# Merge statistics in one group of products, and residual gate rows computed beside the first projections

## The chip, the cores and the metric

The kernel runs on one core of a Trainium2 chip. The core has TensorE (PE) for matrix products, VectorE (DVE), ScalarE (ACT) and GpSimd (POOL) for the rest, SyncE (SP), which issues the kernel's transfers here, and 16 DMA engines that carry them. Each of these works through its own instructions in order and waits on semaphores for the others. The metric is the device time of one execution in microseconds (us), as the median of the runs; the profile and its trace come from one execution more.

## The reference

One step of a one-layer decoder with two parallel branches, width 1024, for 512 prompt rows and 8 x 4 sample rows:

```python
shift, scale, gate = split(silu(c) @ w_cond + b_cond)
h = x * (1 + scale) + shift
qa, ka, va, za, qkv_b, zb, a_b, b_b, g_a, g_b = split(h @ w_in)
yA = combine_groups(dilated softmax attention, 3 head groups) * silu(za)
yB = rmsnorm(gated delta rule over 8 heads of 128) * silu(zb)
merged = sigmoid(g_a) * (yA @ w_branch_a) + sigmoid(g_b) * (yB @ w_branch_b)
x = layernorm(ALPHA * x + gate * (merged @ w_out))
```

`gate` is the residual gate: one row of 1024 values for the prompt and one for each of the 8 sample sequences (`c_prompt` and `c_sample` have nine rows together). `combine_groups` weighs the three groups' attention outputs by their shares of the softmax denominator; for that the kernel needs each query's maximum and sum of every group: the merge statistics. All is in float32.

## The kernel before, in words

The kernel doesn't issue its instructions in the order in which the Python text names them. Calls on the engine objects are recorded (class `Recorder`, L244); generator threads record their part piece by piece, taking turns by rank and due time (class `Threads`, L680: among the parts that are due, the one with the smaller rank goes first, and a `yield 4.0` asks to come back 4 us later by the planner's own count). Then `schedule` (L425) puts every engine's instructions in one fixed order with a cost model, and `emit` writes them; so every instruction of the trace shows line 670, and work is told apart by the names of its tiles. Operations recorded within `rec.together()` (L331) stay contiguous on their engine; others may have instructions of other threads put between them.

The main thread is `stream` (L905, rank 9): the input projections, then the branch products. A job is 48 matmuls, 8 blocks of the contraction times three passes of high and low parts (`hhi`, `hlo` by `hi`, `lo`) for each of two halves of 272 columns, into two PSUM banks `pp` in turn. The weights come as `wt` (512 KB) into three buffers; ACT makes `hi` and DVE `lo` from them. A bank comes free when its half is evacuated, for the gate jobs `za` and `zb` by a tanh on ACT and `zt<-zt,pp` on DVE. Beside the stream run the attention (`prompt_attention`, L1405), the delta rule of eight heads (tiles `kq`, `KQ`, `NTs`, `QKd`, `S`, `rc`, results `dO`), the sample rows, and copies of the caches (`out_kv_s`).

After the attention pairs j = 1 and j = 3, `prompt_attention` merges the groups (L1504 to L1540). It turns the statistics `st` into rows with 40 small products, each two records in the trace, into one bank `pt` (a `pg` bank): four kinds `kd` of statistics, in four strips of PE columns at 0, 32, 64 and 96 (`tile_position`). For each kind and each strip r, the even kinds have four products and the odd ones a single one. On DVE and ACT follows a chain over `R` and `Z` that ends in the weights `R`; these go to DRAM (`dw<-R`, L1527, four transfers) and come back broadcast over 64 partitions each (`wv<-dw`, L1534, eight transfers); `ya` and `NB` are multiplied by them and added (L1537 to L1539). The event `merged[j]` is set then, and the job `za` for j (L1867) starts on it.

The residual gate rows come from `gate_rows` (L1956), a thread of rank 1 that is added for the last phase (L2112), beside the branch products. It loads the bias rows into `gp` (128 equal rows for the prompt) and `gs` (64 rows for the samples), and for each half of 512 columns loads the gate's part of `w_cond` in four transfers of 512 KB (`wc`, from a pool of its own), multiplies it with the conditioning (`cs`) in two groups of 4 products, into a `pd` bank of 32 rows, copies it to `Y`, and spreads the rows with two selector products: `selc` for `gp`, `selg` for `gs`, with an addition on DVE after each. `gp` and `gs` are read in the layer's last stage (from L2153 on), which multiplies the output products with them.

The tiles named `o` (pool `op`, nine buffers of 128 x 544) hold, later on, the gate jobs' `zt`, `ybh` and the low parts `yal`.

Of the kernel before, what the change touches and what calls it, by code (L numbers as in the profile page):

```python
# [11 lines left out]
F32 = mybir.dt.float32  # L12
# [7 lines left out]
D = 1024  # L20
KT = 8
# [4 lines left out]
NT = SEQ + NS  # L26
# [48 lines left out]
def shape_constants():  # L75

    p = np.arange(128)
    b4, i4, h8 = p // 32, p // 8 % 4, p % 8
    blk = {}
    blk["ident"] = np.eye(128)  # L80
    blk["selc"] = (p[:, None] % 32 == np.arange(9)[None, :])
    tok = np.arange(2 * NS)
    blk["selg"] = (p[:, None] % 32 == 1 + tok[None, :] % NS // 4)
    blk["triu"] = (p[:, None] <= p[None, :])
    same = p[:, None] // 4 == p[None, :] // 4
    blk["btri"] = same & (p[:, None] <= p[None, :])
    blk["bones"] = same
    blk["low16"] = np.where(p[:, None] % 32 >= 16, -1.0, 0.0)
    blk["strict4"] = same & (p[:, None] < p[None, :])
    blk["dmask"] = np.where(p[:, None] <= p[None, :], 0.0, -BIG)  # L90
    blk["dmask_s"] = np.where(same & (p[:, None] <= p[None, :]), 0.0, -BIG)
    blk["bmask"] = (p[:, None] % 32 // 4 == np.arange(8)[None, :])
    blk["hmask"] = (p[:, None] % 4 == np.arange(4)[None, :])
    sab = np.zeros((128, 4, 4))
    for h4 in range(4):
        for g in range(2):
            sab[4 * g + h4::16, h4, g] = 1.0
            sab[8 + 4 * g + h4::16, h4, 2 + g] = 1.0
    blk["selab"] = sab.reshape(128, 16)
    blk["sel16"] = p[:, None] % 16 == np.arange(16)[None, :]  # L100
    cols, blobs = {}, []
    for names in (("ident", "selc", "selg", "low16", "dmask"), ("selab", "sel16", "triu", "btri", "bones"),
                  ("strict4", "dmask_s", "bmask"), ("hmask",)):
        at = 0
        for name in names:
            cols[name] = (at, blk[name].shape[1])
            at += blk[name].shape[1]
        blobs.append(np.ascontiguousarray(np.concatenate([blk[n] for n in names], axis=1), dtype=np.float32))
    return cols, blobs


CCOLS, CONST = shape_constants()
# [131 lines left out]
class Recorder:  # L244
# [20 lines left out]
    def pool(self, make, name, bufs, side):  # L265
        return Pool(self, make, name, bufs, side)
# [456 lines left out]
def body(ctx, tc, io):  # L723
    rec = Recorder()
    pe, ve, se, ge, sp = rec.engines()
    mv = sp
    threads = Threads(rec)

    pool = lambda stack, name, bufs, side="left": stack.enter_context(rec.pool(
        lambda: tc.tile_pool(name=name, bufs=bufs, side=side, reuse_waits="tile"), name, bufs, side))  # L730
# [12 lines left out]
    dram = ctx.enter_context(rec.pool(lambda: tc.tile_pool(name="dram", bufs=1, space=DRAM), "dram", 1, "dram"))  # L743

    def pg():
        return psg.tile([128, 512], F32, name="pg", tag="g")

    def pd():
        return psd.tile([128, 512], F32, name="pd", tag="d")
# [4 lines left out]
    def pp():  # L754
        return psp.tile([128, 512], F32, name="pp", tag="pp")


    cst = consts.tile([128, CONST[0].shape[1]], F32, name="cst")
    tables = {"early": cst}

    def take(gen, n):
        for _ in range(n):
            if next(gen, "end") == "end":
                return

    def C(name, where="early"):
        a, n = CCOLS[name]
        return tables[where][:, a:a + n]

    ident = C("ident")  # L770
# [11 lines left out]
    op = pool(octx, "opool", 9, "right")  # L782
# [12 lines left out]
    def cond_product(part, load, ps):  # L795


        for k, n, wc in load(part):
            q = (k + 2 * n) % 4
            pe.matmul(ps[n][32 * q:32 * q + 32, :], cs[:, k, :], wc, start=(k < 4), stop=(k >= 4),  # L800
                      tile_position=(0, 32 * q))
            yield

    def cond_rows(part, k0, nk):
        return io["w_cond"][k0 * 128:(k0 + nk) * 128, part * D:(part + 1) * D].rearrange("(k p) c -> p k c", p=128)

    def to_features(pv, k, rows):

        for i in range(4):
            pe.matmul(pv[:, k + i, 0:9], rows[:, 128 * i:128 * i + 128], C("selc"), start=True, stop=True)  # L810
# [16 lines left out]
    with ExitStack() as fctx:  # L827
# [36 lines left out]
        for part, t in ((1, sc), (0, sh)):  # L864
            ps = [pp(), pp()]
# [3 lines left out]
            for n in range(2):  # L869
                Y = fr.tile([128, 512], F32, name="Y", bufs=2)  # L870
                if n:
                    se.activation(Y, ps[n], AF.Copy)
                else:
                    ve.tensor_copy(Y, ps[n])
                to_features(pv, 4 * n, Y)
            if part:
# [94 lines left out]
    tail = d0.tile([128, 34], F32, name="tail")  # L971
    etot = d0.tile([128, 34], F32, name="etot")
    dO = dram.tile([8, 128, 512], F32, name="dO")
    qd = dram.tile([2, 2, NS, 256], F32, name="qd")
    us = d0.tile([128, 3, 8, NS], F32, name="us")
    oS = keep.tile([128, 8, NS], F32, name="oS")
# [428 lines left out]
    def prompt_attention():  # L1405

        for j in range(4):
            qt, kt, vrow = {}, {}, {}
            for g in range(3):
# [3 lines left out]
                pt = pg()  # L1413
# [4 lines left out]
                pt = pg()  # L1418
# [5 lines left out]
                for u, t in enumerate((krow, vrow[g])):  # L1424
                    if g == 0:
                        sp.dma_start(io["kv0_p"][:, u, cs_], t[:, 3])
                    else:
                        o = io[f"kv{g}_p"].rearrange("(n a r) u c -> a n r u c", a=4, r=4)
# [4 lines left out]
            if j % 2 == 0:  # L1433
                NB = ap.tile([128, 2, 512], F32, name="NB")
                st = ap.tile([128, 4, 4, 4], F32, name="st")
# [29 lines left out]
            for i in range(4):  # L1465
# [5 lines left out]
                for hh in range(2):  # L1471
                    pt = pg()
# [30 lines left out]

            pt = pg()  # L1504
            ve.memset(pt, 1.0)
            for kd in range(4):
                for r in range(4):
                    o = pt[32 * r:32 * r + 4, 128 * kd:128 * kd + 128]
                    if kd % 2:
                        pe.matmul(o, st[:, kd, r, :], ident, start=True, stop=True, tile_position=(0, 32 * r))  # L1510
                        continue
                    for i in range(4):
                        pe.matmul(o.rearrange("p (a n) -> p n a", a=4)[:, 8 * i:8 * i + 8, :], st[:, kd, i, :],
                                  ident[:, r:128:4], start=True, stop=True, tile_position=(0, 32 * r))
            R = ap.tile([128, 4, 128], F32, name="R", tag="P", bufs=2)
            Z = ap.tile([128, 4, 128], F32, name="Z", tag="P", bufs=2)
            two = lambda t: t[:, None, :].to_broadcast([128, 2, 128])
# [10 lines left out]
            for j2 in (j - 1, j):  # L1528
                wv = []
                for u in range(2):  # L1530
                    w = ap.tile([128, 512], F32, name="wv", tag="PT" if j2 < j else "P", bufs=2)
# [423 lines left out]

    def gate_rows():  # L1956

        b = io["b_cond"][:, 2 * D:]
        sp.dma_start(gp, b.to_broadcast([128, D]))
        sp.dma_start(gs, b.to_broadcast([64, D]))  # L1960
        ps = [pd(), pd()]
        yield 4.0
        for n in range(2):
            w = slice(512 * n, 512 * n + 512)

            for k0 in range(0, KT, 4):
                wc = []
                for k in (k0, k0 + 2):
                    wc.append(wcp.tile([128, 2, 512], F32, name="wc"))
                    sp.dma_start(wc[-1], cond_rows(2, k, 2)[:, :, w])  # L1970
                with rec.together():
                    take(cond_product(2, lambda part: ((k0 + k, n, wc[k // 2][:, k % 2]) for k in range(4)), ps), 99)
                yield 2.0
            Y = zp.tile([128, 512], F32, name="Y", tag="rbo")
            se.activation(Y, ps[n], AF.Copy)
            yield 1.8
            for t, r, sel in ((gp, 128, C("selc")[:, 0:1].to_broadcast([128, 128])), (gs, 64, C("selg"))):
                p = pg()
                pe.matmul(p[0:r], sel, Y, start=True, stop=True)
                ve.tensor_add(t[:, w], t[:, w], p[0:r])  # L1980


    for s in (1, 0, 2):
# [33 lines left out]
    def early():  # L2017
        yield freed[1], merged[1]
        t, slabs = early_tiles()
        sample_queries(0, slabs()[0:64, 0:256], t["qr"])  # L2020
        yield from sample_attention(0, t, slabs, 512, 6.0, (ve,), early_over)
        yield tuple(ready[3, g] for g in range(3))
        sample_queries(1, slabs()[0:64, 0:256], qr1)

    threads.add(early(), 4)

    def prep():
# [15 lines left out]
    zp = pool(zctx, "zp", 2, "right")  # L2043
# [32 lines left out]
    gp = al.tile([128, D], F32, name="gp")  # L2076
    gs = al.tile([64, D], F32, name="gs")
# [12 lines left out]
            se.activation(wo[n][0][:, k:k + 2], raw, AF.Copy)  # L2090
            ve.tensor_sub(wo[n][1][:, k:k + 2], raw, wo[n][0][:, k:k + 2].bitcast(F32))

    wctx = ExitStack()
    wcp = pool(wctx, "wcp", 3, "right")

    def merge_after(m):
        def after():
            t = gate_tile["ga", m]
# [10 lines left out]

    for m in range(8):  # L2110
        jobs += [gate_job("ga", m)] * (m >= EARLY_A) + [branch_job("ga", m, 4, of_a, after=merge_after(m))]
    threads.add(gate_rows(), 1)  # L2112
    threads.add(stream(len(jobs)), 9)
    threads.run(lambda: not threads.parts)
    wctx.close()
    zctx.close()
    gates_ctx.close()
    octx.close()
# [15 lines left out]
    r = [o1.tile([128, D], F32, name=f"r{tt}") for tt in range(5)]  # L2134
# [18 lines left out]
    for n in range(2):  # L2153
        for tt in (4, 0, 1, 2, 3):
# [8 lines left out]
            for c in range(512 * n, 512 * n + 512, step):  # L2163
                po = product_out(tt, c, c + step)
                w = slice(c, c + step)
# [15 lines left out]
            w, w2 = slice(0, m), slice(m, 1024)  # L2181
# [118 lines left out]
```

## Time and profile before

| what | value |
|---|---|
| runs | 942.03, 938.55, 942.79 us; median 942.03 |
| profiled execution | 939.77 us, its span 938.0 us |
| mean granted PE clock | 0.984 |
| moved by DMA | 237.76 MB, mean 253 GB/s |

How to read the rows of the trace: in the rows of the order of time stand the start in us from the span's start, the time of the row, engine, line, operation, what it writes and reads, its shape, how many instructions the row holds, and in brackets how long the engine had been idle and who released it. "SPq" rows are the issue of a transfer, not the transfer. Rows of waits have: who waited, for whom, us in all, times, the longest. A matmul's own time overlaps with that of the next, so that its cost is read from the distance of starts.

### The profile page before, as it was taken

To read this page: it belongs to the slowest core of one execution; us is meant where nothing else is said; L and a number is where in the kernel's file an instruction comes from. 1 tells how busy PE (TensorE), PEld (TensorE's weight loads), DVE (VectorE), ACT (ScalarE), POOL (GpSimd) and SP (SyncE) were. 2 spreads that over 40 slices of the span, in tenths; PEclk is the share of its full clock that TensorE was granted. 3 is DMA by queue.
4 is the path that set the end of the run, shared out by engine and by line. 5 is a ranking of instruction groups with operands and counts; after the bars stand their busy time and mean duration, and the time that the engine had idled before them with its cause. 6 is when DMAs were issued, how large, how long until landed. Compare 5 with 4: busy or idle time off the path is not lost.

```text
span 938.0 us, 20669 instructions
## 1 busy us (share of the span) xinstructions
PE 892.0 (95%) x8070; PEld 825.8 (88%) x8070; DVE 736.8 (79%) x1620; ACT 417.0 (44%) x975; POOL 64.0 (7%) x176
## 2 busy tenths in 40 slices
PE   4799999999999999999999998988999999999995
PEld 1599999999989999979999997877999999998784
DVE  1575556876799999889989997556899789957768
ACT  0365347753557443576725753441532222234411
POOL 0120000200011110010100200001020000000000
PEclk9799999999999999999999999998999999999998
DMA  9677773658878778786787868459689899988613
GB/s 357 226 220 238 221 246 136 224 182 251 272 249 273 229 250 287 236 292 219 241 301 242 277 206 298 140 172 365 219 267 360 340 418 377 361 284 306 205 43 112
DMA packets 106341, 237.76 MB, mean 253 GB/s; under 512 B 30898, under 2 KB 62140, under 8 KB 103556
## 3 DMA queue, kind: packets, MB, share of 16 engines
q1 hardware_dynamic: 106244, 236.45, 73.8%
q8 instruction: 63, 1.03, 0.4%
q14 instruction: 34, 0.28, 0.1%
HBM read 220.40 MB, written 103.70 MB: 346 GB/s over the span
## 4 chain that ended last, share of the span: by engine, by line
PE 72%; DVE 11%; DMA 4%; ACT 3%; issue 2%; SPq 0%; POOL 0%; DVEq 0%; POOLq 0%; ACTq 0%
PE pp L670 55%; PE pg L670 7%; PE pd L670 6%; PE pb L670 3%; DVE slab L670 2%; DMA dO<-orow 1%; DMA wv<-dw 1%; DMA slab<-in_vs 1%; DVE lo L670 1%; ACT L670 1%; DVE XF L670 1%; DVE r L670 1%; ACT hi L670 1%; DVE ya L670 1%; DVE acc L670 0%
## 5 line engine op out<-in xcount | busy, mean ns | idle before, releaser
L670 PE MATMUL pp<-hhi,hi 128*128 128x272 f32 x1408 | 415.6, 295 | 11.3 <-DVE zt L670 8.7
L670 PE MATMUL pp<-hhi,lo 128*128 128x272 f32 x1408 | 415.3, 295 | 0.0
L670 PE MATMUL pp<-hlo,hi 128*128 128x272 f32 x1408 | 414.1, 294 | 0.2 <-DVE small L670 0.2
L670 PEld LDWEIGHTS pp<-hhi,hi 128*128 128x128 f32 x1408 | 267.2, 190 | 13.7 <-DVE zt L670 9.1
L670 PEld LDWEIGHTS pp<-hlo,hi 128*128 128x128 f32 x1408 | 267.2, 190 | 2.7 <-issue 0.9
L670 PEld LDWEIGHTS pp<-hhi,lo 128*128 128x128 f32 x1408 | 266.5, 189 | 3.3 <-issue 1.8
L670 ACT ACTIVATE hi<-wt 128x1024 fp32r<-128x1024 f32 (+1 forms) x104 | 106.8, 1027 | 167.7 <-PE pp L670 144.8
L670 DVE TENSOR_TENSOR lo<-wt,hi 128x1024 fp32r<-128x1024 f32 (+1 forms) x104 | 122.5, 1178 | 54.8 <-ACT hi L670 54.0
L670 DVE SCALAR_TENSOR_TENSOR acc<-ext,cw,acc 128x568 f32<-128x568 f32 x72 | 57.5, 799 | 0.7
L670 ACT ACT_TABLE_LOAD x38 | 48.8, 1283 | 9.3 <-DMA cT<-in_cT 8.0
L670 DVE TENSOR_TENSOR slab<-slab 128x512 f32<-128x512 f32 (+1 forms) x66 | 42.4, 663 | 3.7 <-DMA slab<-in_vs 3.1
L670 DVE TENSOR_REDUCE slab<-slab 128x8 f32<-128x512 f32 (+2 forms) x66 | 42.4, 655 | 0.3
L670 ACT ACTIVATE P<-P,st 128x256 f32<-128x256 f32 (+1 forms) x64 | 31.3, 491 | 19.7 <-DVE st L670 19.5
L670 PE MATMUL pp<-ybl,hi 128*128 128x272 f32 x128 | 37.0, 289 | 0.0
L670 PE MATMUL pp<-ybh,lo 128*128 128x272 f32 x128 | 37.0, 289 | 0.0
L670 PE MATMUL pp<-ybh,hi 128*128 128x272 f32 x128 | 36.8, 288 | 0.0
L670 ACT ACTIVATE zt<-pp 128x272 f32<-128x272 f32 x48 | 18.4, 389 | 34.7 <-PE pp L670 31.7
L670 POOL COPY cx<-ext 128x3 f32<-128x3 f32 (+1 forms) x48 | 23.3, 515 | 94.0 <-ACT ext L670 93.9
L670 ACT ACTIVATE vn<-pd,beta 128x128 f32<-128x128 f32 x32 | 11.7, 366 | 34.4 <-PE pd L670 34.3
L670 DVE TENSOR_TENSOR Tb<-Tb,tmp 32x15 f32<-32x15 f32 (+7 forms) x120 | 23.4, 195 | 4.1
L670 PE MATMUL pp<-wc,cs 128*32 128x512 f32 x64 | 13.1, 916 | 14.3 <-DMA wc<-in_w_cond 14.3
L670 ACT ACTIVATE ext<-pp 128x272 f32<-128x272 f32 (+2 forms) x72 | 20.0, 314 | 14.9 <-PE pp L670 13.9
(395 smaller groups left out, 1574.3 us busy)
## 6 DMA issues: line engine op xcount, KB each, us to landing
out_kv_s<-in_cache SPq DMA_DIRECT2D x144, 512.0 KB
wt<-in_w_in SPq DMA_DIRECT2D x88, 512.0 KB
out_kv_s<-in_cache SPq DMA_DIRECT2D x24, 496.0 KB
wc<-in_w_cond SPq DMA_DIRECT2D x8, 1024.0 KB
slab<-in_ks SPq DMA_DIRECT2D x32, 256.0 KB
slab<-in_vs SPq DMA_DIRECT2D x32, 256.0 KB
kv<-in_ks SPq DMA_DIRECT2D x16, 512.0 KB
kv<-in_vs SPq DMA_DIRECT2D x16, 512.0 KB
```

The lines of the kernel that those rows point to most:

```text
L670: getattr(real[x.engine], x.name)(*map(arg, x.args), **{k: arg(v) for k, v in x.kw.items()})
```

## The change

The merge's 40 products are recorded within `rec.together()`, and the loops stand in another order: kind, product, strip, so that four successive products go to the four column strips in turn. The products themselves are the same.

`gate_rows` is added beside `early()`, before the first projections, as a thread of rank 5. For each half of the columns it loads the weights in eight transfers of 256 KB (`wg`) into `o` tiles that nothing else uses at that time, does the eight products in one group, and copies the result to `Y`. A single selector product of 73 columns (9 of `selc`, 64 of `selg`, which are neighbours in the constants) makes the rows of both kinds at once. The bias comes as a transfer that broadcasts one row of 512 values over 73 partitions (`grow`), DVE adds the product to it, and a transfer stores the 73 rows in a DRAM tile `dg`. At the place where the thread was added before, `gp` is loaded from `dg`'s first row, broadcast, and `gs` from its rows 9 to 72. The pool `wc` of the late weights is gone. From the removed lines on, line numbers are up to four smaller than before.

```diff
+    dg = dram.tile([73, D], F32, name="dg")
...
             pt = pg()
             ve.memset(pt, 1.0)
-            for kd in range(4):
-                for r in range(4):
-                    o = pt[32 * r:32 * r + 4, 128 * kd:128 * kd + 128]
-                    if kd % 2:
-                        pe.matmul(o, st[:, kd, r, :], ident, start=True, stop=True, tile_position=(0, 32 * r))
-                        continue
-                    for i in range(4):
-                        pe.matmul(o.rearrange("p (a n) -> p n a", a=4)[:, 8 * i:8 * i + 8, :], st[:, kd, i, :],
-                                  ident[:, r:128:4], start=True, stop=True, tile_position=(0, 32 * r))
+            with rec.together():
+                for kd, i in ((kd, i) for kd in range(4) for i in range(1 if kd % 2 else 4)):
+                    for r in range(4):
+                        o = pt[32 * r:32 * r + 4, 128 * kd:128 * kd + 128]
+                        if kd % 2:
+                            pe.matmul(o, st[:, kd, r, :], ident, start=True, stop=True, tile_position=(0, 32 * r))
+                        else:
+                            pe.matmul(o.rearrange("p (a n) -> p n a", a=4)[:, 8 * i:8 * i + 8, :], st[:, kd, i, :],
+                                      ident[:, r:128:4], start=True, stop=True, tile_position=(0, 32 * r))
...
     def gate_rows():
 
-        b = io["b_cond"][:, 2 * D:]
-        sp.dma_start(gp, b.to_broadcast([128, D]))
-        sp.dma_start(gs, b.to_broadcast([64, D]))
-        ps = [pd(), pd()]
-        yield 4.0
+        sel = cst[:, CCOLS["selc"][0]:CCOLS["selc"][0] + 73]
         for n in range(2):
             w = slice(512 * n, 512 * n + 512)
-
-            for k0 in range(0, KT, 4):
-                wc = []
-                for k in (k0, k0 + 2):
-                    wc.append(wcp.tile([128, 2, 512], F32, name="wc"))
-                    sp.dma_start(wc[-1], cond_rows(2, k, 2)[:, :, w])
-                with rec.together():
-                    take(cond_product(2, lambda part: ((k0 + k, n, wc[k // 2][:, k % 2]) for k in range(4)), ps), 99)
-                yield 2.0
-            Y = zp.tile([128, 512], F32, name="Y", tag="rbo")
+            wc = [op.tile([128, NT], F32, name="wg", tag="o")[:, 0:512] for _ in range(KT)]
+            for k in range(KT):
+                sp.dma_start(wc[k], io["w_cond"][128 * k:128 * k + 128, 2 * D + 512 * n:2 * D + 512 * n + 512])
+            ps = {n: pd()}
+            yield 6.0
+            with rec.together():
+                take(cond_product(2, lambda part: ((k, n, wc[k]) for k in range(KT)), ps), 99)
+            Y = op.tile([128, NT], F32, name="Y", tag="o")[:, 0:512]
             se.activation(Y, ps[n], AF.Copy)
-            yield 1.8
-            for t, r, sel in ((gp, 128, C("selc")[:, 0:1].to_broadcast([128, 128])), (gs, 64, C("selg"))):
-                p = pg()
-                pe.matmul(p[0:r], sel, Y, start=True, stop=True)
-                ve.tensor_add(t[:, w], t[:, w], p[0:r])
+            rows = op.tile([128, NT], F32, name="grow", tag="o")[0:73, 0:512]
+            sp.dma_start(rows, io["b_cond"][:, 2 * D + 512 * n:2 * D + 512 * n + 512].to_broadcast([73, 512]))
+            yield 3.0
+            p = pd()
+            pe.matmul(p[0:73], sel, Y, start=True, stop=True)
+            ve.tensor_add(rows, rows, p[0:73])
+            sp.dma_start(dg[:, w], rows)
+            yield 1.0
...
+    threads.add(gate_rows(), 5)
     threads.add(early(), 4)
...
-    threads.add(gate_rows(), 1)
+    sp.dma_start(gp, dg[0:1].to_broadcast([128, D]))
+    sp.dma_start(gs, dg[9:73])
     threads.add(stream(len(jobs)), 9)
     threads.run(lambda: not threads.parts)
-    wctx.close()
```

More of the change, by code (lines that the diff above doesn't have):

```diff
@@ L2091, in load_out @@
             ve.tensor_sub(wo[n][1][:, k:k + 2], raw, wo[n][0][:, k:k + 2].bitcast(F32))
-    wctx = ExitStack()
-    wcp = pool(wctx, "wcp", 3, "right")
     def merge_after(m):
```

## The prediction

> **What bounds the kernel now.** I read the page first, then PE's waits, the stretches around the longest one, and last the order of work on DVE and SP there.
>
> ```profile
> span 938.0 us, 20669 instructions
> PE 892.0 (95%) x8070; PEld 825.8 (88%) x8070; DVE 736.8 (79%) x1620; ACT 417.0 (44%) x975; POOL 64.0 (7%) x176
> ...
> PE pp L670 <- DMA wc<-in_w_cond: 14.3, 6, 10.6
> PE pp L670 <- DVE zt L670: 9.2, 2, 8.7
> ```
>
> PE is busy for 95% of the span. So whatever takes PE time away in a full stretch is a gain at its whole length, and whatever makes PE wait in one is a loss at its whole length. The first wait, 14.3 us, is the conditioning at the start, which the change doesn't touch. The second is one stall of 8.7 us:
>
> ```profile
> 627.67 1.02 PE L670 MATMUL pb<-kq 128*128 128x256 f32 x4
> 637.44 0.59 PE L670 MATMUL pp<-hhi,hi 128*128 128x272 f32 x1 [8.75 <-DVE zt L670]
> ...
> 637.40:641.00 3.60, 3.56 (x16) 3.56 (x17) 2.14 (x7) 0.00 (x0) 2.03 (x5) 0.50 1.14 348
> ...
> 81.00:96.00 15.00, 15.00 (x120) 14.88 (x119) 8.14 (x17) 4.77 (x9) 0.00 (x0) 1.00 0.65 208
> ```
>
> After it the granted clock is 0.50 for 3.6 us: 16 matmuls take 3.6 us, 0.225 each, where a full stretch at clock 1.00 has 120 in 15 us, 0.125 each: another 1.6 us. (The columns of such rows: the stretch and its length, busy time and count of PE, PEld, DVE, ACT and POOL, the granted clock, the DMA share, GB/s.) The stall with its tail costs 10.4 us. What DVE and SP did before it:
>
> ```profile
> 612.18 1.31 PE L670 MATMUL pg<-cst,st 128*4 128x32 f32 x32
> ...
> 619.81 0.43 DVE L670 TENSOR_TENSOR R<-R,Z 128x256 f32<-128x256 f32 x1
> 620.26 2.81 SPq L670 DMA_DIRECT2D dw<-R  x4
> 625.03 4.97 SPq L670 DMA_DIRECT2D wv<-dw  x8
> 630.54 1.02 DVE L670 TENSOR_TENSOR ya<-ya,wv 128x512 f32<-128x512 f32 x1 [0.48 <-DMA wv<-dw]
> 636.96 0.78 DVE L670 SCALAR_TENSOR_TENSOR zt<-zt,pp 128x272 f32<-128x272 f32 x2
> ```
>
> This is the second merge of the attention branch. The statistics products end at 613.49, DVE works out R until 620.24, R goes to DRAM and comes back broadcast, and the ya operations run from 630.54. The evacuation `zt<-zt,pp`, which frees PE's bank, stands behind them in DVE's order.
>
> **The change part by part. (1) Statistics products together.** Today the planner cuts the second merge's products into pieces over 9.2 us, with projections and delta-rule products between; the first merge's stay whole:
>
> ```profile
> 604.29 1.08 PE L670 MATMUL pg<-cst,st 128*4 128x32 f32 x28
> ...
> 608.96 0.28 PE L670 MATMUL pp<-hhi,lo 128*128 128x272 f32 x1
> 609.17 0.38 PE L670 MATMUL pg<-cst,st 128*4 128x128 f32 x2
> 609.48 0.49 PE L670 MATMUL pd<-S,KQ 128*128 128x128 f32 x2
> ...
> 306.38 2.65 PE L670 MATMUL pg<-cst,st 128*4 128x32 f32 x80
> ```
>
> From 608.96 to 609.48 are 0.52 us, of which the projection needs 0.125: a piece of two records costs 0.39. Whole, 80 records take 2.65 us, 0.07 for two. Four such pieces (I leave the longer ones' edges out) save 4 x 0.32 = 1.3 us.
>
> The larger part: begun at 604.29, the whole group ends at 606.94 and not at 613.49. R's chain, which hangs on it, moves 6.5 us ahead; the projections that stood between come behind it. PE's work up to the blocked matmul shrinks by the 1.3 us alone, so it blocks at about 628.7 - 1.3 = 627.4 and is freed at 637.44 - 6.5 = 630.9: 3.5 us instead of 8.75. A wait of that size stands earlier in the trace:
>
> ```profile
> PE pg L670 <- DVE st L670: 3.1, 1, 3.1
> ...
> 578.70:582.10 3.40, 3.30 (x30) 2.27 (x31) 2.87 (x11) 2.32 (x9) 0.00 (x0) 0.63 0.98 347
> ```
>
> It too has a tail: 3.4 us at 0.63, 1.3 us lost; I take 1.4. Gain 10.4 - 4.9 = 5.5. Bounds: R's way through DRAM took 10.3 us here, 620.24 to 630.54, but 14.4 in the first merge, where the reciprocal's product ended at 328.78 and `ya<-ya,wv` began at 343.17:
>
> ```profile
> 328.38 0.40 DVE L670 TENSOR_TENSOR R<-R,Z 128x256 f32<-128x256 f32 x1
> 343.17 1.07 DVE L670 TENSOR_TENSOR ya<-ya,wv 128x512 f32<-128x512 f32 x1 [0.54 <-DMA wv<-dw]
> ```
>
> With 4.1 us more the gain is 1.4; at most it is 10.4, the stall gone. The order of the products, with the four column strips in turn, leaves their number and sizes; the trace has no such order. If a group took half or twice its 2.65 us, the two merges would gain 2.7 or lose 5.3; I take nothing, since the pieces of today change strips too.
>
> **(2) Gate rows leave the late stage.** There PE is full, so its products count whole:
>
> ```profile
> 839.26 0.29 PE L670 MATMUL pp<-yah,hi 128*128 128x272 f32 x1
> 839.48 1.06 PE L670 MATMUL pd<-wc,cs 128*32 128x512 f32 x8
> 840.70 0.29 PE L670 MATMUL pp<-yah,lo 128*128 128x272 f32 x1
> ...
> 852.56 1.02 PE L670 MATMUL pg<-Y,cst 128*128 128x512 f32 x2
> ...
> 855.00:872.00 17.00, 17.00 (x123) 13.53 (x122) 12.39 (x22) 9.36 (x16) 0.00 (x0) 1.00 0.83 297
> ```
>
> A group of 8 records costs 840.70 - 839.26 - 0.25 = 1.19 us, four of them 4.8; the two records of a selector product take 1.02, four products 4.1. Removed: 8.9. The new place, beside the first projections, is as full (below), so there the products count whole too: two groups of 16 records, 2.2 each (two of 1.19 less one pair of edges), and two selector products with 73 columns, 1.02 each: 6.4, or up to 8.9 if each group is cut in two. Gain 2.5, at the least nothing. The `Y` copies on ACT, the additions on DVE and the late loads lay beside that full PE: nothing; at the new place the same holds for ACT (4.77 us busy of the 15 after 81.00), not for DVE's additions (3). `gp` and `gs` are read back from `dg` where PE is full, and are read only in the layer's last stage; without that cover 0.75 MB would show with about 2 us at the 407 GB/s below.
>
> **(3) The new transfers.** The eight loads of 512 KB late give way to sixteen of 256 KB early. The first eight fall where DMA has nothing to do, the next into a loaded stretch:
>
> ```profile
> 28.00:30.00 2.00, 1.02 (x8) 0.16 (x8) 0.29 (x1) 0.31 (x1) 0.72 (x4) 1.00 1.05 407
> ...
> 36.00:38.00 2.00, 1.87 (x8) 1.87 (x9) 2.00 (x7) 0.18 (x1) 0.07 (x1) 0.50 0.56 143
> 38.00:44.00 6.00, 6.00 (x42) 5.87 (x41) 5.09 (x10) 3.10 (x6) 1.10 (x3) 0.81 0.00 0
> ...
> 66.00:81.00 15.00, 14.86 (x116) 14.51 (x115) 8.89 (x20) 11.18 (x30) 1.35 (x5) 1.00 0.70 227
> ```
>
> The first eight, 2 MB, take 5 us at 407 GB/s, in the six in which nothing moves: free. The others add 2 MB where 0.70 and 0.65 of the engines' time is taken: 5 us out of 10 free ones. What is new in kind are four transfers of 73 rows of 2 KB: the bias broadcast into `grow`, and `grow` out to `dg`, once for each half. Two small transfers alone in a window show how rows are shared out:
>
> ```profile
> 63.61 0.69 SPq L670 DMA_DIRECT2D drows<-rows  x2
> ...
> DMA packets 21, 0.03 MB, mean 28 GB/s; under 512 B 10, under 2 KB 12, under 8 KB 20
> ```
>
> In 64.30 to 65.20 they carry their 8 rows of 2 KB and 2 of 512 B, and ten packets of under 512 B more: one short packet for each row, as if 8 rows went over 8 engines and 2 over 2, each closing by itself. So a transfer is cut into equal shares of rows. 73 is prime: its one equal cut is a single engine. A full engine moves 407/16 = 25.4 GB/s, so 73 x 2048 bytes take 5.9 us on one, and 0.4 us if spread over 16. Of these ends I take 5.9. All other transfers have a sixteenth of their bytes behind it on that engine, and land as late.
>
> The Trainium skill says the same outright ("DMA: Bandwidth & Descriptors", section "Why a DMA increments its semaphore by 16 and not by 1"): the engines are the largest number up to 16 that divides the outermost dimension of both sides, and 127 partitions get 1. The window agrees for 8 and 2 rows; no run yet shows 73. By that rule too the four take one engine.
>
> What waits, in the changed order of each engine:
>
> ```profile
> 71.99 0.20 DVE L670 RECIPROCAL rc<-rc 128x8 f32<-128x8 f32 x1 [0.82 <-ACT rc L670]
> 87.47 0.68 DVE L670 TENSOR_TENSOR QKd<-NTs,rb 128x512 f32<-128x512 f32 x1
> ...
> 75.78 0.30 SPq L670 DMA_DIRECT2D dr<-rrow  x1
> 80.32 0.34 SPq L670 DMA_DIRECT2D rb<-dr  x1
> ```
>
> The first `grow` is issued at about 65.5, once the first group of products has freed a tile, and lands about 74. Its DVE addition stands ahead of the reciprocal of `rc`, and PE's `pb<-rc` behind that: PE has the group until 66.9, then 40 projections, a selector product and four transposes, 6.5 us, and wants `rc` at 73.4; it is there at 75.1: 1.7 us lost. On SP the store to `dg` stands ahead of the eighth `wg` load, of `dr` and `rb`; it waits for that addition (74.5). The engine then has its share of 3 MB (7 `wg`, bias, `wt`, `cr`: 7.6 us) and the 5.9 of the store: the eighth `wg` lands about 88. PE wants it 51 projections and a pair of `pb` after 75.3, at 82.2: 5.8 lost, and 1.6 of half clock. `dr` lands about 91, `rb` about 95, the second `grow` about 101. Its addition stands ahead of `QKd<-NTs,rb`, which now runs at 87.47, and PE's next `pb` pair waits for the evacuations behind it: 4.2 and 1.4 lost. Sum 1.7 + 7.4 + 5.6 = 14.7. At 0.4 us a transfer, none of these waits is over 1 us. The `wt` loads survive the delay: one issued at 66.27 is first read at 84.63, 18 us later:
>
> ```profile
> 66.27 0.37 SPq L670 DMA_DIRECT2D wt<-in_w_in  x1
> 84.63 1.06 ACT L670 ACTIVATE hi<-wt 128x1024 fp32r<-128x1024 f32 x1 [2.87 <-PE pp L670]
> ```
>
> **Sum.** Gains 1.3 + 5.5 + 2.5 = 9.3, loss 14.7: +5.4. The profiled execution took 939.77 us (span 938.0), so 945.2; the median of the three runs, 942.03, lies 2.3 above it, so 947.4 is what runs should show.
>
> **Rivals.** (a) The 73 rows spread over the engines, or the cover is wider than I think: the loss is at most 1 us, the gains stand: 942.0 - 8.3 = 933.7, and with the stall wholly gone (4.9 more) 929. This one ends on the other side, and it decides from about 2 us a transfer downwards, where the loss is 14.7 x 2/5.9 = 5 and 4.3 of the 9.3 are left. For it: the loss hangs on a row that shows 8 and 2, not 73. Against: the equal cut. (b) The early waits are as I say and the merge's stall stays, R's way taking 14.4 us as in the first merge: the gain in (1) shrinks from 5.5 to 1.4, and 951.5 comes out. For it: `wv<-dw` now falls into other loads. (c) The two waits behind `grow` are hidden by slack in DVE's work for head 0, so only the 7.4 at the second group remains: 942.0 - 9.3 + 7.4 = 940.1, no change to be told. For it: DVE is busy for only 8.9 of the 15 us after 66.00. Against: both its waits are for DMA, which a free DVE doesn't shorten.
>
> **How the numbers follow.** Under 0.5%, 4.7 us, a run of this kernel can't be told from no change. Forecast 0.56, (a) 0.24, (b) 0.12, (c) 0.08. The forecast's own range, waits of 10 to 24 us in all (at most the 4 x 5.9 of the transfers, at least two thirds of my sum), is 942.7 to 956.7; 0.17 of its 0.56 I put within 0.5%, below 946.7, and 0.39 above. Faster: (a) and a quarter of (c), 0.26. Slower: (b) and 0.39 less a little for rounding, 0.50. Same: the rest, 0.24. The range 930 to 959 leaves out the best of (a) and the worst of (b) with the longest waits.
>
> **What would show it.** Right: PE gaps near 74, 82 to 90 and 98 to 106, with a granted clock under 1 behind them; a time from issue to landing of `grow` and `dg` of 6 us or more; DVE idle ahead of `grow<-grow,pd`; the second merge's products as one row of 80 and PE's wait on `zt` under 5 us. Wrong: PE full from 64 to 110, or the wait on `zt` still over 8 us.

## The result, and the profile after

The changed kernel takes 943.67 us (median of 20 runs) where the kernel before takes 940.73 (median of 20 beside it): ratio 1.0029, 95% interval 1.0019 to 1.0039. It is slower by 2.9 us; the prediction had 5.4 and 947.4. The profiled execution took 942.16 us, its span 940.4. From the page of the changed kernel, and its list of PE's waits (us in all, times, the longest):

```profile
span 940.4 us, 20668 instructions
PE 889.6 (95%) x8066; PEld 824.9 (88%) x8066; DVE 734.6 (78%) x1618; ACT 419.0 (45%) x977; POOL 75.1 (8%) x176
...
PE pb L670 <- DVE QKd L670: 6.5, 2, 6.0
PE pg L670 <- ACT P L670: 4.0, 2, 2.5
PE pd L670 <- DMA wg<-in_w_cond: 2.7, 1, 2.7
PE pb L670 <- DVE rc L670: 2.6, 1, 2.6
...
PE pp L670 <- DVE spare L670: 2.1, 1, 2.1
```

PE is busy 2.4 us less than before and idle 4.8 us more. The wait of 8.7 us on `zt` is gone, 2.1 on `spare` stand in its place; the 4.0 on `P` stand in the place of 3.1 on `st`. New are three waits that were foretold: on `rc`, on the eighth `wg` and on `QKd`. In PE's order of time, and the DVE and SP rows behind them:

```profile
76.02 0.27 PE L670 MATMUL pb<-cst,rc 128*8 128x128 f32 x1 [2.62 <-DVE rc L670]
...
88.77 1.04 PE L670 MATMUL pd<-wg,cs 128*32 128x512 f32 x2 [2.65 <-DMA wg<-in_w_cond]
...
104.57 2.08 PE L670 MATMUL pb<-KQ 128*128 128x256 f32 x4 [5.96 <-DVE QKd L670]
```

```profile
74.87 0.68 DVE L670 TENSOR_TENSOR grow<-grow,pd 73x512 f32<-73x512 f32 x1 [3.83 <-DMA grow<-in_b_cond]
...
100.99 0.68 DVE L670 TENSOR_TENSOR grow<-grow,pd 73x512 f32<-73x512 f32 x1 [6.28 <-DMA grow<-in_b_cond]
...
64.85 0.42 SPq L670 DMA_DIRECT2D grow<-in_b_cond  x1
77.87 0.24 SPq L670 DMA_DIRECT2D dg<-grow  x1
90.20 0.33 SPq L670 DMA_DIRECT2D rb<-dr  x1
90.58 0.28 SPq L670 DMA_DIRECT2D grow<-in_b_cond  x1
```

The bias rows need 10 us each time, from the issue at 64.85 to the addition at 74.87 and from 90.58 to 100.99. At the end of the second, nothing else moves. The DMA view of the stretch from 98 to 100 us:

```profile
DMA packets 24, 0.05 MB, mean 25 GB/s; under 512 B 0, under 2 KB 0, under 8 KB 24
...
q1 hardware_dynamic: 24, 0.05, 6.5%
```

Twelve rows of 2 KB per us, 25 GB/s, a share of 6.5%: one engine of sixteen, as the sum had it. At 12 rows per us the 73 take 6 us: in the trace the packets of 2 KB of the second load follow each other from 94.48 to 100.40, and the first starts 3.9 us after the issue.

At the second merge the group is whole, and shorter than any before:

```profile
618.76 1.57 PE L670 MATMUL pg<-cst,st 128*4 128x32 f32 x80
...
643.16 0.39 PE L670 MATMUL pp<-hhi,hi 128*128 128x272 f32 x1 [2.11 <-DVE spare L670]
```

80 records take 1.57 us, where the first merge before took 2.65.

### The profile page after: what moved, and what is told of

The parts are those of the page before. It is cut to its first block, busy times and chain, and to the rows that moved or that the text cites. A ratio compares the mean times of both kernels' runs of the same rounds, so it can differ in the third digit from the quotient of the medians.

```text
span 940.4 us, 20668 instructions
## 1 busy us (share of the span) xinstructions
PE 889.6 (95%) x8066; PEld 824.9 (88%) x8066; DVE 734.6 (78%) x1618; ACT 419.0 (45%) x977; POOL 75.1 (8%) x176
## 4 chain that ended last, share of the span: by engine, by line
PE 72%; DVE 11%; DMA 10%; ACT 2%; issue 2%; SPq 2%; DVEq 0%; ACTq 0%
PE pp L670 56%; PE pg L670 8%; PE pd L670 6%; PE pb L670 3%; DMA wc<-in_w_cond 2%; SPq L670 2%; DMA dr<-rrow 2%; DVE lo L670 2%; DMA wg<-in_w_cond 1%; DMA grow<-in_b_cond 1%; DMA slab<-in_vs 1%; DVE slab L670 1%; DVE Tb L670 1%; DVE tmp L670 1%; DVE r L670 1%
## 5 line engine op out<-in xcount | busy, mean ns | idle before, releaser
L670 POOL COPY cx<-ext 128x3 f32<-128x3 f32 (+1 forms) x48 | 33.7, 732 | 88.4 <-ACT ext L670 88.4
L670 ACT ACTIVATE spare<-pp 128x272 f32<-128x272 f32 (+1 forms) x32 | 16.0, 499 | 26.2 <-PE pp L670 26.1
L670 PE MATMUL pg<-cst,P 128*128 128x128 f32 x120 | 22.9, 284 | 4.2 <-ACT P L670 4.0
```

The costliest lines, as they stand in the source:

```text
L670: getattr(real[x.engine], x.name)(*map(arg, x.args), **{k: arg(v) for k, v in x.kw.items()})
```

## The experiments

Each run was timed in five rounds beside the kernel before. Times are medians; the ratios are to before, with their 95% intervals.

**How many rows the four transfers have.** Three kernels change nothing but this.

The first has 80 rows in all four:

```diff
-    dg = dram.tile([73, D], F32, name="dg")
+    dg = dram.tile([80, D], F32, name="dg")
...
-            rows = op.tile([128, NT], F32, name="grow", tag="o")[0:73, 0:512]
-            sp.dma_start(rows, io["b_cond"][:, 2 * D + 512 * n:2 * D + 512 * n + 512].to_broadcast([73, 512]))
+            rows = op.tile([128, NT], F32, name="grow", tag="o")[0:80, 0:512]
+            sp.dma_start(rows, io["b_cond"][:, 2 * D + 512 * n:2 * D + 512 * n + 512].to_broadcast([80, 512]))
...
-            ve.tensor_add(rows, rows, p[0:73])
+            ve.tensor_add(rows[0:73], rows[0:73], p[0:73])
```

> The bias rows and dg have 80 rows instead of 73 (seven rows more than needed, never read), in all four transfers; everything else is as in the changed kernel. Theory (73 rows go through one DMA engine, 80 go through 16): PE's waits on rc (2.6 us), on the eighth wg (2.7) and on QKd (6.0) and the 1.8 us of half clock behind the last are gone, 13 us less than the changed kernel's 943.7: about 931, ratio to before near 0.989. DVE's idle ahead of grow<-grow,pd, 10.1 us in two, falls under 1.5. Rival (the waits come from the 2 MB of wg in a loaded stretch and from the place of the additions in DVE's order, not from the number of rows): within 2 us of the changed kernel, 942 to 945, and DVE's waits for grow stay over 6 us.

Measured: 930.19 us, 0.9879 (0.9852 to 0.9905), profiled span 926.5. Of DVE's waits for `grow` 1.8 us are left and of PE's on `QKd` 1.7; those on `rc` and `wg` are gone:

```profile
DVE grow L670 <- DMA grow<-in_b_cond: 1.8, 1, 1.8
...
PE pb L670 <- DVE QKd L670: 1.7, 2, 1.4
```

Against the changed kernel that is 0.0150 of 941, 14.1 us, for seven rows more per transfer that nobody reads. The place of the loads and the 2 MB of weights are not what costs. The version is faster than both kernels.

The second has 80 rows in the two loads alone:

```diff
-            rows = op.tile([128, NT], F32, name="grow", tag="o")[0:73, 0:512]
-            sp.dma_start(rows, io["b_cond"][:, 2 * D + 512 * n:2 * D + 512 * n + 512].to_broadcast([73, 512]))
+            rows = op.tile([128, NT], F32, name="grow", tag="o")[0:80, 0:512]
+            sp.dma_start(rows, io["b_cond"][:, 2 * D + 512 * n:2 * D + 512 * n + 512].to_broadcast([80, 512]))
...
-            ve.tensor_add(rows, rows, p[0:73])
-            sp.dma_start(dg[:, w], rows)
+            ve.tensor_add(rows[0:73], rows[0:73], p[0:73])
+            sp.dma_start(dg[:, w], rows[0:73])
```

> Only the two bias loads have 80 rows; the stores to dg keep 73. Theory (one engine for 73 rows): DVE's first wait for grow is gone and PE's 2.6 on rc with it; the store still holds one engine for 6 us ahead of the eighth wg, dr and rb, but is issued 3 us sooner: 3 to 6 us of waits stay, about 936. Rival (the number of rows is nothing): 942 to 945.

Measured: 934.81, 0.9921 (0.9898 to 0.9945). As expected; the loads carry most of the cost. PE's wait on `wg` is 1.3 us and on `QKd` 2.2.

The third splits the two stores alone:

```diff
-            sp.dma_start(dg[:, w], rows)
+            sp.dma_start(dg[0:64, w], rows[0:64])
+            sp.dma_start(dg[64:73, w], rows[64:73])
```

> Only the stores are changed: rows 0 to 63 and rows 64 to 72 of each half go in two transfers (64 and 9 rows); the loads keep 73. Theory (64 rows go over 16 engines, 9 over 9): the first wait on rc stays (2.6 us), the eighth wg comes in time, rb and the second grow are issued some 6 us sooner, which leaves 2 to 4 us of waits in all: about 934. Rival (what waits is the load of grow alone, the store delays nothing): the wait on QKd stays at 5 to 6, about 941.

Measured: 941.40, 1.0004 (0.9988 to 1.0020): the theory's 934 missed, the rival's 941 met. The wait on `wg` is gone, but those on `rc` (3.5) and `QKd` (4.6) stay: the second `grow` is issued at 85.22, over 5 us sooner than in the changed kernel, and its addition still waits until 97.56. A load that something waits for pays the queue ahead of it on its one engine and then its own 6 us; a store delays only what stands behind it.

A fourth asks how the rows are cut, with 74 = 2 x 37 in all four transfers:

```diff
-    dg = dram.tile([73, D], F32, name="dg")
+    dg = dram.tile([74, D], F32, name="dg")
...
-            rows = op.tile([128, NT], F32, name="grow", tag="o")[0:73, 0:512]
-            sp.dma_start(rows, io["b_cond"][:, 2 * D + 512 * n:2 * D + 512 * n + 512].to_broadcast([73, 512]))
+            rows = op.tile([128, NT], F32, name="grow", tag="o")[0:74, 0:512]
+            sp.dma_start(rows, io["b_cond"][:, 2 * D + 512 * n:2 * D + 512 * n + 512].to_broadcast([74, 512]))
...
-            ve.tensor_add(rows, rows, p[0:73])
+            ve.tensor_add(rows[0:73], rows[0:73], p[0:73])
```

> As the kernel with 80 rows, with 74 in the four transfers. Theory (equal cuts: 74 = 2 x 37 go through two engines, 3 us a transfer, between 73's 5.9 and 80's 0.4): the waits of 13.5 us that 73 rows cost over 80 fall to 4 to 7, 934 to 937, with PE's wait on QKd at 2 to 4 us. Rival (only multiples of 16 or 8 are spread, all else goes to one engine): 942 to 945. Second rival (only primes go to one engine): 930.

Measured: 936.76, 0.9949 (0.9929 to 0.9969), in the middle. PE's wait on `QKd` is 3.8 us in all, its longest 3.4. The addition behind the second bias load:

```profile
94.38 0.69 DVE L670 TENSOR_TENSOR grow<-grow,pd 73x512 f32<-73x512 f32 x1 [3.68 <-DMA grow<-in_b_cond]
```

The bias rows can be told in the trace by their packets of 2 KB. The 74 start within 3.3 us, 90.39 to 93.73, 12 in each half us, where the 73 of the changed kernel come at 6 in each half us: two engines for one. The first load of the kernel with 80 rows has its 80 packets within 1.3 us, 67.83 to 69.10, up to 14 of them under way at once. So neither "primes go to one, all else to sixteen" nor "only multiples of 8 are spread" holds: equal cuts do. The rule of the Trainium skill named in the prediction ("DMA: Bandwidth & Descriptors", "Why a DMA increments its semaphore by 16 and not by 1") gives 1, 2 and 16 engines for 73, 74 and 80 rows. The traces agree for one and two; for 80 rows they show at least 14.

**The bias rows ahead of the weights.** From the kernel with 80 rows:

```diff
+            rows = op.tile([128, NT], F32, name="grow", tag="o")[0:80, 0:512]
+            sp.dma_start(rows, io["b_cond"][:, 2 * D + 512 * n:2 * D + 512 * n + 512].to_broadcast([80, 512]))
             wc = [op.tile([128, NT], F32, name="wg", tag="o")[:, 0:512] for _ in range(KT)]
...
-            rows = op.tile([128, NT], F32, name="grow", tag="o")[0:80, 0:512]
-            sp.dma_start(rows, io["b_cond"][:, 2 * D + 512 * n:2 * D + 512 * n + 512].to_broadcast([80, 512]))
```

> The kernel with 80 rows (930.2), with each half's bias rows loaded ahead of its weights instead of behind its products. Theory (what is left of the waits for grow is the place of the load in the queue): DVE's remaining 1.8 us ahead of the second addition and PE's 1.4 on QKd vanish: 928 to 929.5. Rival (PE then waits for the next thing, the weights themselves or rb): 930 to 931.

Measured: 929.71, 0.9877 (0.9852 to 0.9902): not told apart from 930.19, and between the theory's range and the rival's. PE's wait on `QKd` fell to 0.8.

**The order of the merge's products.** The changed kernel with its products grouped in the old order:

```diff
             with rec.together():
-                for kd, i in ((kd, i) for kd in range(4) for i in range(1 if kd % 2 else 4)):
-                    for r in range(4):
+                for kd in range(4):
+                    for r in range(4):
...
+                        for i in range(4):
```

> The changed kernel with the merge's products in one group, but in the order of before (kind, strip, product: four products of a strip in succession). Theory (it is the order with the four strips in turn that shortened a group from 2.65 us in the first merge before to 1.57 after): groups of 80 records take 2.65 again, the time is 2.2 us over the changed kernel's, about 945.9. Rival (the 1.57 comes from another cause, the group's surroundings): groups stay at 1.6 and the time within 0.5 us.

Measured: 948.69, 1.0081 (1.0055 to 1.0106), 5.0 us over the changed kernel. The second merge there:

```profile
619.64 2.66 PE L670 MATMUL pg<-cst,st 128*4 128x32 f32 x80
```

The order makes the group's length, 1.57 or 2.66, 1.1 us for each merge. That is 2.2 of the 5.0. The rest isn't explained. Behind the first merge the plan has another order; but up to there both kernels have the same instructions in the same order on every engine, and the profiled execution here is 1.9 us behind that of the changed kernel already at 119 us (its wait on `rc`, at about 76 us, is 3.6 us instead of 2.6).

**The merge's part and the gate rows' part alone.** The kernel before with the merge's part of the diff, and nothing of the gate rows:

```diff
+            with rec.together():
-            for kd in range(4):
-                for r in range(4):
+                for kd, i in ((kd, i) for kd in range(4) for i in range(1 if kd % 2 else 4)):
+                    for r in range(4):
...
```

> The kernel before with the merge's part of the change alone; the gate rows are computed in the late stage as before. Theory (the merge's part gains 1.3 us of pieces, 2.2 of the strips in turn and some 6 of the stall with its tail): 9.5 us under before, about 932, PE's wait on zt or spare at the second merge under 3.5 us, both groups of 80 records at 1.6 us. Rival (most of what the run with 80 rows gained, 11.2 us, came from the gate rows' move, and the merge gave little because the stall only moves to other evacuations): 937 to 940.

Measured: 944.78, 1.0033 (1.0014 to 1.0052). The theory missed by 13 us, and the rival too. The stream does end sooner: the first output product starts at 866.18, in the kernel before at 875.08. Some 3.2 us of that are only put off: one group of late gate products and its selectors, which stood ahead of the output products before and stand behind their first here:

```profile
866.18 0.40 PE L670 MATMUL pp<-wo0h,ms 128*64 128x512 f32 x1
...
875.54 1.07 PE L670 MATMUL pd<-wc,cs 128*32 128x512 f32 x8
877.33 2.13 PE L670 MATMUL pg<-Y,cst 128*128 128x512 f32 x4 [0.72 <-ACT Y L670]
885.56 0.77 PE L670 MATMUL pp<-wo0h,mhi 128*128 128x512 f32 x1 [6.11 <-DVE lo L670]
...
885.50:889.00 3.50, 3.44 (x8) 2.82 (x9) 3.50 (x5) 2.24 (x3) 0.00 (x0) 0.50 0.45 161
```

The planner has put the last group of late gate products and its selectors among the output products. PE then waits 6.1 us and runs at half clock. To see whether the gain is there, the same kernel with another rank for the late gate rows, which puts the group ahead of the output products:

```diff
-    threads.add(gate_rows(), 1)
+    threads.add(gate_rows(), 0)
```

> The run with the merge's part alone (944.8) once more, with the late gate rows as a thread of rank 0 instead of 1; in the planned order the last group of gate products then stands ahead of the output products and not among them. Theory (the merge's part gains 8.8 us by the time the stream ends, and loses 12 after it because the last gate products come late, with 6.7 us of wait for wo1l and half clock behind): 932, at most 935, the wait of 6.1 us on lo gone. Rival (the output stage itself can't begin earlier, since its weights come late): 940 or more.

Measured: 935.55, 0.9940 (0.9920 to 0.9960). The 6.1 us wait is gone and 9 us are back; of the 8.8 expected under before, 5.3 came; the 8.8 had counted the 3.2 us that were only put off. So the merge's part gains by itself, and its first run gave that back in the output stage. No run has rank 0 with the merge as before, so a share of the rank itself isn't ruled out.

The two halves of it, each alone on the kernel before: grouped in the old order, and the new order without the group.

```diff
+            with rec.together():
-            for kd in range(4):
-                for r in range(4):
+                for kd in range(4):
+                    for r in range(4):
...
```

> The kernel before with the merge's products grouped, in their old order of kind, strip, product. Theory of the prediction (the whole group lets R's chain start 6.5 us sooner): 6.8 us under before, 934 to 935, and the wait on zt falls from 9.1 to under 4 us. Rival (the planner puts the group elsewhere in PE's order, and the strips in turn made the difference): 939 to 944 with the wait on zt over 6.

Measured: 936.43, 0.9953 (0.9932 to 0.9973). The group stands whole, and the wait on `zt` is halved:

```profile
602.43 2.66 PE L670 MATMUL pg<-cst,st 128*4 128x32 f32 x80
...
PE pp L670 <- DVE zt L670: 4.5, 1, 4.5
```

```diff
-            for kd in range(4):
-                for r in range(4):
+            for kd, i in ((kd, i) for kd in range(4) for i in range(1 if kd % 2 else 4)):
+                for r in range(4):
...
```

> The kernel before with the products in the new order of kind, product, strip, not grouped. Theory (the strips in turn shorten a whole group from 2.65 to 1.57 us; the second merge's pieces gain less): 1 to 2 us under before, 939 to 940, the 8.7 us stall stays. Rival (the new order alone moves the plan so that the stall goes too): 932 to 935.

Measured: 937.95, 0.9960 (0.9941 to 0.9979), more than 1 to 2 us and less than the rival's. The second merge is still in pieces, and still the wait on `zt` falls to 5.4:

```profile
602.44 0.98 PE L670 MATMUL pg<-cst,st 128*4 128x32 f32 x46
604.99 0.46 PE L670 MATMUL pg<-cst,st 128*4 128x32 f32 x17
607.49 0.77 PE L670 MATMUL pg<-cst,st 128*4 128x32 f32 x17 [2.04 <-issue]
...
PE pp L670 <- DVE zt L670: 5.4, 2, 5.0
```

The other way round, the gate rows' part with the merge as before, with 73 rows and with 80 (the changed kernel, and the one with 80 rows, less the merge's part):

```diff
-            with rec.together():
-                for kd, i in ((kd, i) for kd in range(4) for i in range(1 if kd % 2 else 4)):
-                    for r in range(4):
+            for kd in range(4):
+                for r in range(4):
...
```

> The changed kernel with the merge's products as before (planner's pieces, kind, strip, product); gate rows early with 73 rows. Theory (2.5 us of PE's work saved, 13 of waits and half clock added by the 73 rows): 10 us over before, about 952, and the 9 us stall on zt is back. Rival (the early waits let DVE and DMA get ahead and are partly given back later): 944 to 948.

> As the run before, with 80 rows in the four transfers. Theory: 2.5 us of PE's work saved less 1 to 2 of remaining waits: 940 (938 to 941). Rival (moving the gate rows costs by its place alone, 2 MB of weights in a loaded stretch): 944 or more.

Measured: 946.36, 1.0056 (1.0034 to 1.0077), and 932.30, 0.9904 (0.9881 to 0.9928). The difference, 14.1 us, is the price of 73 rows a second time. Both are lower than their theories, by 6 and 8 us; the first lies in its rival's range. In the trace of the one with 80 rows there is no wait on `zt` at all, though the merge's products are still cut by the planner. PE's and DVE's order of time around the second merge:

```profile
603.34 1.31 PE L670 MATMUL pg<-cst,st 128*4 128x32 f32 x36 [1.15 <-issue]
604.96 0.97 PE L670 MATMUL pg<-cst,st 128*4 128x32 f32 x26
606.90 0.84 PE L670 MATMUL pg<-cst,st 128*4 128x32 f32 x12
...
631.59 0.39 PE L670 MATMUL pp<-hhi,hi 128*128 128x272 f32 x1 [1.89 <-DVE spare L670]
```

```profile
623.94 1.06 DVE L670 TENSOR_TENSOR ya<-ya,wv 128x512 f32<-128x512 f32 x1 [0.47 <-DMA wv<-dw]
624.91 0.42 DVE L670 SCALAR_TENSOR_TENSOR spare<-spare,pp 128x272 f32<-128x272 f32 x1
626.39 1.06 DVE L670 TENSOR_TENSOR NB<-NB,wv 128x512 f32<-128x512 f32 x1
...
631.08 0.45 DVE L670 SCALAR_TENSOR_TENSOR spare<-spare,pp 128x272 f32<-128x272 f32 x1
```

Two things differ from the kernel before. First, the statistics stand earlier in PE's order. Counted in the matmul records that write `pp`, 5136 in each kernel's trace, the statistics begin behind 3102 of them, in the kernel before behind 3161, and the first `ya` runs when 3188 have started, in the kernel before 3280. Second, an evacuation stands between the `ya` and `NB` operations, at 624.91, and the next at 631.08, where before all eight operations stood ahead of it. The move of the gate rows shifted the plan by enough for both, 500 us later. No run separates the two.

| kernel | merge as before | merge grouped, strips in turn |
|---|---|---|
| gate rows late | 940.7 | 944.78; 935.55 with rank 0 |
| gate rows early, 73 rows | 946.36 | 943.67 |
| gate rows early, 80 rows | 932.30 | 930.19 |

## Why the prediction was right and wrong, point by point

**The transfers of 73 rows: right in mechanism, and in the sum.** One engine each, all three waits at their places, in the order foretold. Forecast 14.7 us, with at most 1 left if the rows were spread; between 73 and 80 rows lie 14.1 and, with the merge as before, 14.3 us by the ratios. The terms are further off than the sum: the wait on `rc` 2.6 for 1.7, on `wg` 2.65 for 5.8 (14 of the group's 16 records run before the missing load, which I had waiting with it), on `QKd` 6.0 for 4.2. Of the two stretches of half clock only the last came, 1.8 us lost for 1.4. That adds up to 13.0; that it lies so near the forecast is in part luck, since errors of both signs cancel.

```profile
88.70:92.00 3.30, 3.23 (x15) 1.86 (x16) 0.00 (x0) 0.60 (x1) 0.00 (x0) 1.00 0.24 93
104.50:108.00 3.50, 3.43 (x11) 2.97 (x12) 2.46 (x7) 0.00 (x0) 0.00 (x0) 0.50 0.35 118
```

**The sum of the gains: the step that failed, in the merge's term.** The traces let the sum be taken by stretches. The table has how much later (+) or earlier (-) than in the kernel before the records that write `pp` start, as the change over each stretch, in us. It rests on one profiled execution of each kernel. The forecast is that for 73 rows: 6.4 and 14.7; 1.3 and 5.5; 8.9.

| stretch of the `pp` records, with its end in the kernel before | forecast | changed kernel | 80 rows | 80 rows, merge as before |
|---|---|---|---|---|
| up to the 600th (118.6 us): the early gate rows | +21.1 | +20.5 | +7.9 | +8.2 |
| up to the 4560th (827.2 us): both merges | -6.8 | -9.4 | -11.1 | -7.5 |
| up to the last (927.4 us): the late gate rows gone | -8.9 | -8.6 | -8.1 | -6.6 |

In the changed kernel the first and the last row hold within 0.6 us. The middle one doesn't: 9.4 us gained for 6.8, and that is about the whole difference between the 5.4 forecast and the 2.9 measured. So the step that failed is the merge's term of the sum, 1.3 + 5.5 with nothing for the strips.

The term put at nothing is the order of the strips, of which the prediction said "I take nothing". It measures 1.1 us a merge on PE, 2.2 in all. My reason, that the pieces of today change strips too, looked past the row I had quoted: the whole group of 80 records, 2.65 us, changes strip only after every fourth product in the even kinds, so it was no price for the new order. The Trainium skill has the rule that I left out ("TensorEngine Tiling (Array Packing)", section "Key Properties"): different tiles of the array work independently, in parallel. 1.57 against 2.66 agrees with it.

The stall's term was off as well: 2.1 us of wait stay, and about 1.7 are lost to the clock behind it (0.67 and 0.84 in the seven us from 643.0), 3.8 for the 4.9 forecast; the waits ahead of it, on `P`, grew instead. So the strips are the right size for the miss, but the runs don't show that they are all of it.

**The stall at the second merge: gone, but for the most part not by the grouping.** I gave 6.8 us to the grouping, since R's chain begins sooner. Alone on the kernel before, the grouping gives 4.4 (936.43), with a wait on `zt` of 4.5 for my 3.5: there the account is fair. In the five kernels with late gate rows PE blocks at the same record, the 3281st that writes `pp`, and the wait falls with the number of them that have started when `ya` begins: 8.75 us at 3280, 5.0 at 3260, 4.5 at 3256, 3.6 at 3249 (two kernels). So an earlier chain does shorten the stall.

In the changed kernel it isn't the grouping that does it: with the gate rows moved, the stall is gone without any grouping (the middle row gains 7.5 us of its 11.1 without the merge's part), and the grouping alone, in the old order, gives nothing on top (948.69 against 946.36, with intervals that overlap). There the plan itself has the statistics earlier, and an evacuation between DVE's operations. I had priced an edit in a plan that stays as it is otherwise; the plan did not stay. That the gains came out within 3 us is luck, then: by the medians, with 80 rows the move of the gate rows gave 9.0 us (1 - 0.9904 of 941) for the 1.5 of the sum (2.5 less 1 of waits), and the merge's part on top of it 2.1 for 6.8.

Of the rivals, (a), the rows are spread, (b), the stall stays as in the first merge, and (c), the waits behind `grow` are hidden, are all refuted by the rows above.

**The gate products: right to about 1 us in each place, with 80 rows.** The first new group runs at once and whole, the second waits for its last weights, and the late ones are gone. With 80 rows the early stretch loses 7.9 us for 6.4 and at most 1 of waits, and the late one gains 8.1 for 8.9. So next to nothing of the 2.5 shows there; with the merge as before the late stretch gains 6.6 alone.

**The base.** The time forecast was hung on a median of 942.03, of three runs; twenty gave 940.73. That is 1.3 of the 3.7 us between 947.4 and 943.67.

What stays open: why the waits ahead of the second merge differ so (3.1 us on `st` in the kernel before, 4.0 on `P` in the changed kernel, 2.3 on `P` with the gate rows' part alone, 1.0 on `st` with the old order), how the other 2.8 us of the old order's 5.0 are made up, and which of the two differences in the plan ends the stall.

## What to carry to other kernels

Look at the number of rows of each transfer: 73 rows cost 14 us where 80 cost almost none, since the row count decides how many engines carry it, and the later transfers' shares on the one engine queue behind it. Small products that go to different column strips should take the strips in turn. Where a planner orders the work, an edit's price read from the old order holds at its own place only; ask which waits are a chance of the order (here how early one chain starts, and one evacuation behind eight operations), because those can go, or come back, with any edit.

## What the runs showed of the hardware that was not expected

Waits of the same length left PE's clock at different rates. After a wait of 3.4 us on `QKd`, in the run with 74 rows, the clock stayed at 1.00; after 3.6 us on `zt`, in the run with rank 0, it was 0.61, and in the kernel before it was 0.63 after 3.1 us. In the changed kernel 2.1 us on `spare` were enough for 0.67, while it stayed at 1.00 after 2.65 on `wg`. The stretches behind the waits in the run with 74 rows, with rank 0 and in the changed kernel:

```profile
98.00:101.50 3.50, 3.50 (x25) 3.34 (x26) 3.36 (x7) 0.53 (x1) 0.00 (x0) 1.00 0.47 112
```

```profile
628.90:632.40 3.50, 3.45 (x18) 3.45 (x19) 1.37 (x5) 0.00 (x0) 2.24 (x4) 0.61 0.94 280
```

```profile
643.00:646.50 3.50, 3.34 (x15) 3.18 (x16) 3.46 (x10) 0.00 (x0) 3.33 (x5) 0.67 0.69 224
```

The Trainium skill ("TensorE: Matmul & The Clock Gate", section "Part 1: The HAM clock gate (the "warmup" mystery)") says that the activity is judged in windows of 3.4 us that run on by themselves; whether a wait about that long fills one depends then on where it falls. The waits of 3.4 and 3.6 us agree with that. Those of 3.1 and 2.1 us don't: they are shorter than such a window, so that they can't fill one, and the clock fell all the same. So the length of a wait alone doesn't foretell it here, and none of the rows shows the windows themselves.
